# Transposed layouts from the host, tile order and buffers in a one-layer hybrid decoder kernel

## The chip, the cores and the metric

The kernel runs on 1 core of one Trainium2 chip. The metric is the device time of one execution in microseconds (us). A profiled execution gives the trace; its span runs from the first to the last instruction.

## The reference

One layer of a hybrid decoder trunk, for 1024 prompt tokens and 8 sample tokens with 4096 cached positions each; model width 1024, all in fp32.

```python
xn = rms_norm(x, norm1_g)
(aq, ak, av, az, ab, aa, bq, bk, bv, iq, ik, iw, ga, gb) = split(xn @ w_in)
# mixer A: causal conv of q, k, v (width 4), SiLU, chunked gated delta rule, gated norm -> oa
# mixer B: indexer scores, top 256 keys per query, softmax attention over them        -> ob
mix = sigmoid(ga) * (oa @ w_out_a) + sigmoid(gb) * (ob @ w_out_b)
h = x + mix @ w_o
hn = rms_norm(h, norm2_g)
y = h + square(relu(hn @ w_up)) @ w_down
```

It returns y, the new K/V and indexer rows, the recurrent state, and the last three rows ahead of the convolution (`conv_prompt`, `conv_sample`).

## The kernel before

Activations lie with channels on the 128 partitions and tokens along the free dimension, in three chunks of 384, 384 and 264 tokens (`CN`; tile t holds 128 tokens, t = 8 is the 8 samples, which stand at the end of chunk 2). Every fp32 operand is split into a high part in the fast fp32r format and a remainder (`split`), and each product is three matmuls. The kernel is written as chains (Python generators) that `Flow.run` interleaves; the planner of the tile framework (line 1867, it schedules with a simulated timeline) then sets the order on each engine. Nearly all loads and stores are issued by SyncE (SP), one queue in order. Since a wrapper issues every engine instruction, the profile gives them all line 83; they are told apart by tile name.

`mixers()` (line 400) comes first. `x_chain` (450) loads token tiles `xt` (two buffers) in the order samples, then 0 to 7; it squares them on ACT, takes the inverse root by Newton steps on VectorE (`rsqrt`, 177; 11 small operations with the mean), scales into a second tile `xs`, transposes (`ptx`, 8 per tile) and splits into `xn`. After the first tile it loads and splits the eight K/V weight blocks (`rawk`, `wk`). `kv_chain` (496) makes keys, values and indexer keys group by group, samples first, and then sets the event that lets the score work start. `dense_chain` runs the indexer queries (`iq_chain`, 938), the convolution part (`a_chain`, 570), queries, gates. `a_chain` transposes the convolution weights and the state on the chip (`ptc`, `pst`) and, at its end, the new convolution rows (`pcv`).

`rest()` (1602) comes second. `mix_a` (1543) projects mixer A's output and multiplies it with the gate, through DRAM (`gd`): for each of eight blocks and each chunk one load (1551), one product and one store (1553). `merge` (1566) follows for the chunks of `FIRST = [2, 0]`, beside the logits and values of the attention, and for `REST = [1]` after them: it loads the attention output (`load_b`, through DRAM), fetches x once more in token order as the residual, transposes it on TensorE (`ptx<-xt`, 8 per tile) and copies it by quarters into `hT` on VectorE and ACT (1572 to 1581); then come the products with `w_out_b` and `w_o`. While the attention runs, the products have one PSUM bank (`pd=1`, 1605). `norm_chain` and `mlp_chain` follow; after the last MLP block `out` (1788) transposes y back to token order (`pty`) and writes it.

Weight blocks come one after the other through `ahead` (1503) and `block` (205): 256 KB into a raw tile (two buffers of tag `raw`; from the MLP's stage on, every third block uses three buffers of tag `ld`, `cur["spare"]`), split by ACT and by VectorE or GpSimd in turn into one of five tiles.

Of the kernel before, what the change touches and what calls it, by code (L numbers as in the profile page):

```python
# [8 lines left out]
F32 = mybir.dt.float32  # L9
# [7 lines left out]
P = 128  # L17
D = 1024
# [12 lines left out]
FIRST, REST = [2, 0], [1]  # L31

# [93 lines left out]
def program(ctx, tc, I, O, dbg=None, upto=99):  # L126
# [78 lines left out]
    def block(src, name, lo="pool", spare=False):  # L205
# [4 lines left out]
        raw = w([P, 512], name + "r", tag="ld", bufs=3, pool=cur["L"]) if spare else \  # L210
# [10 lines left out]

    def cs(j):
        return slice(C0[j], C0[j] + CN[j])

    def dense(ws, xin, evac, chunks=range(3)):

        for j in chunks:
            p = pst("pdn", "pd")
# [117 lines left out]

    def q_rows(t, gt):
# [52 lines left out]
    def mixers():  # L400
# [49 lines left out]
        def x_chain():  # L450
# [9 lines left out]
            load(8)  # L460
            g1 = w([P, D], "g1")
            dma(g1, I["norm1_g"].to_broadcast([P, D]))
            load(0)
            wt["gt"] = gains(pools["A"])
            dma(gng, I["gdn_norm_g"].rearrange("a p -> p a"))
            wk = w([P, 2, KT, 336], "wk", F32R)
            for i, t in enumerate(order):
                n = NS if t == 8 else P
                x_ = xt[t]
                xs = w([P, D], "xs", bufs=2)  # L470
                ss = small([P, 1], "ss")
                S.activation(xs[:n], x_[:n], AF.Square, accum_out=ss[:n])
                V.tensor_scalar(ss[:n], ss[:n], 1.0 / D, EPS, op0=OP.mult, op1=OP.add)
                rs = small([P, 1], "rs")
                rsqrt(rs[:n], ss[:n])
                V.scalar_tensor_tensor(xs[:n], x_[:n], rs[:n], g1[:n], op0=OP.mult, op1=OP.mult)
                if i + 2 < 9:
                    load(order[i + 2])
                for j in range(2):
                    pt = pst("ptx", "px")  # L480
                    p3 = pt[:, :4 * n].rearrange("p (k n) -> p k n", k=4)
                    for k in range(4):
                        T.transpose(p3[:, k, :], xs[:n, (4 * j + k) * P:(4 * j + k + 1) * P], ident[:n, :n])
# [3 lines left out]
                if t == 8:  # L487
                    for k in range(KT):
                        raw = wts.tile([P, 512], F32, name="rawk", tag="raw", bufs=WB[1])
                        dma(raw[:, :336], I["w_kv"][:, k])  # L490
                        split(wk[:, 0, k], wk[:, 1, k], raw[:, :336], "act", "dve")
                    wt["kv"] = [wk[:, :, k] for k in range(KT)]
                    flow.set(ev_wkv)
# [76 lines left out]
        def a_chain():  # L570
            cur["p"] = pools["A"]
            cwr = w([48, P], "cwr", tag="j2", bufs=5, pool=C)
            dma(cwr, I["conv_w"][0].rearrange("j (t p) -> (j t) p", p=P))
            ptc = pst("ptc", "pt")
            T.transpose(ptc[:, :48], cwr, ident[:48, :48])
            cw = w([P, 4, 12], "cw")
            V.tensor_copy(cw, ptc[:, :48].rearrange("p (j t) -> p j t", j=4))
            stT = w([P, 12, 24], "stT")
            for g3 in range(3):
                scr = w([24, 512], "scr", tag="j2", bufs=5, pool=C)  # L580
                for j in range(3):
                    dma(scr[8 * j:8 * j + 8], I["state_conv"][0, :, j, g3 * 512:(g3 + 1) * 512])
                pt = pst("pst", "pt")
                for q in range(4):
                    T.transpose(pt[:, q * 24:(q + 1) * 24], scr[:, q * P:(q + 1) * P], ident[:24, :24])
                V.tensor_copy(stT[:, 4 * g3:4 * g3 + 4], pt[:, :96].rearrange("p (t x) -> p t x", t=4))
            dma(O["conv_sample"][0, :, 0:2, :], I["state_conv"][0, :, 1:3, :])
# [56 lines left out]
            for g3 in range(3):  # L644
                pcv = pst("pcv", "pt")
# [1233 lines left out]
```

## Time and profile before

| | us |
|---|---|
| median of 3 runs | 1876.12 |
| lowest, highest | 1874.29, 1876.82 |
| the profiled execution | 1872.74 |
| its span | 1870.9 |

The profile's page gives each engine's busy time, and the same in 40 slices of the span; stage tables, timelines and tile views are cut from the same trace. PE is TensorE's matmul, PEld its weight load, DVE VectorE, ACT ScalarE, POOL GpSimd, SP SyncE.

### The profile page before, as it was taken

What the parts mean: (1) busy time and instruction counts of PE and PEld (TensorE: products, weight loads), DVE (VectorE), ACT (ScalarE), POOL (GpSimd) and SP (SyncE); (2) the same over time, 40 slices, a digit from 0 to 9 for tenths busy, and PEclk for the clock granted to TensorE, in tenths of its full rate; (3) what the DMA queues carried; (4) which work ended last, traced back from release to release, by engine and by line L of the source; (5) the groups of instructions that cost most, each with busy time, mean ns of one, the idle gap of its engine ahead of it and who ended that gap; (6) DMA issues with size and microseconds to landing.
All of it is one profiled execution on the core that took longest, in us unless ns stands there. A gap on an engine that the chain in (4) does not pass through costs nothing.

```text
span 1870.9 us, 32909 instructions
## 1 busy us (share of the span) xinstructions
PE 1790.5 (96%) x11966; PEld 1715.5 (92%) x11966; DVE 1091.9 (58%) x2956; ACT 830.3 (44%) x1917; POOL 613.8 (33%) x765
## 2 busy tenths in 40 slices
PE   6999988899999999999899889999999999999998
PEld 4899978799898999989789889999999999999998
DVE  7868767998988896177778785323232323232323
ACT  4456684566687532256657544121313131313131
POOL 2434235613422362221443655121312131313130
PEclk9999999999999999999899999999999999999999
DMA  5325464225445444554654452111111111111112
GB/s 174 129 94 178 130 213 121 84 66 151 121 133 149 136 145 120 186 166 122 205 167 148 133 169 79 52 50 47 46 46 46 52 45 51 47 46 46 46 35 91
DMA packets 167764, 199.30 MB, mean 107 GB/s; under 512 B 29521, under 2 KB 112769, under 8 KB 167594
## 3 DMA queue, kind: packets, MB, share of 16 engines
q1 hardware_dynamic: 163314, 183.57, 32.4%
q0 software_dynamic: 4288, 13.64, 2.5%
q8 instruction: 94, 1.54, 0.3%
q14 instruction: 68, 0.56, 0.1%
HBM read 149.51 MB, written 47.73 MB: 105 GB/s over the span
## 4 chain that ended last, share of the span: by engine, by line
PE 45%; DMA 2%; DVE 2%; POOL 1%; issue 1%; ACT 0%; SPq 0%; ACTq 0%; POOLq 0%; DVEq 0%
PE pdn L83 42%; PE po L83 1%; PE ptp L83 1%; PE pat L83 1%; PE pty L83 0%; POOL wc L83 0%; DMA wc28r<-in_w_o 0%; DMA wc64r<-in_w_o 0%; DVE rs L83 0%; DVE wc L83 0%; DMA ld<-obd 0%; PE ptx L83 0%; DVE ga L83 0%; POOL ssq L83 0%; DMA wc58r<-in_w_b 0%
## 5 line engine op out<-in xcount | busy, mean ns | idle before, releaser
L83 PE MATMUL pdn<-u,wc 128*128 128x384 f32 (+1 forms) x2304 | 367.4, 320 | 0.0
L83 PEld LDWEIGHTS pdn<-u,wc 128*128 128x128 f32 x2304 | 362.8, 188 | 0.1
L83 PE MATMUL pdn<-hn,wc 128*128 128x384 f32 (+1 forms) x2304 | 362.1, 319 | 0.0
L83 PEld LDWEIGHTS pdn<-hn,wc 128*128 128x128 f32 x2304 | 360.5, 188 | 0.3
L83 DVE TENSOR_TENSOR hT<-hT,pdn 128x384 f32<-128x384 f32 (+1 forms) x216 | 110.5, 512 | 247.5 <-PE pdn L83 244.4
L83 PE MATMUL pdn<-xn,wu 128*128 128x384 f32 (+1 forms) x1440 | 250.8, 325 | 0.9 <-ACT z L83 0.9
L83 PEld LDWEIGHTS pdn<-xn,wu 128*128 128x128 f32 x1440 | 224.7, 189 | 9.1 <-issue 4.6
L83 DVE SCALAR_TENSOR_TENSOR r<-pdn,rs 128x384 f32<-128x384 f32 (+1 forms) x96 | 49.4, 515 | 273.6 <-PE pdn L83 273.5
L83 POOL TENSOR_TENSOR u<-r,u 128x384 fp32r<-128x384 f32 (+1 forms) x96 | 89.3, 931 | 274.1 <-ACT u L83 247.5
L83 PE MATMUL pa<-xn,wu 128*128 128x384 f32 (+1 forms) x864 | 160.2, 331 | 0.8 <-ACT a L83 0.8
L83 PEld LDWEIGHTS pa<-xn,wu 128*128 128x128 f32 x864 | 141.9, 195 | 3.2 <-ACT a L83 1.1
L83 ACT ACTIVATE r<-r 128x384 f32<-128x384 f32 (+1 forms) x96 | 47.1, 492 | 172.3 <-DVE r L83 171.6
L83 ACT ACTIVATE jka<-sc,nf 128x512 bf16<-128x512 f32 (+3 forms) x124 | 101.4, 822 | 27.0 <-DVE nf L83 21.5
L83 PE MATMUL pdn<-mix,wc 128*128 128x384 f32 (+1 forms) x576 | 100.6, 328 | 4.5 <-DVE wc L83 2.2
L83 PEld LDWEIGHTS pdn<-mix,wc 128*128 128x128 f32 x576 | 94.5, 194 | 7.8 <-ACT mix L83 2.6
L83 DVE SCALAR_TENSOR_TENSOR a<-u,cw,a 128x384 f32<-128x384 f32 (+1 forms) x108 | 76.0, 706 | 9.1 <-ACT a L83 8.1
L83 POOL TENSOR_TENSOR wu<-wu_4r,wu 128x512 fp32r<-128x512 f32 x32 | 42.2, 1318 | 92.6 <-ACT wu L83 77.7
L83 DVE TENSOR_SCALAR_CACHE_REDUCE jk<-sc,cf 128x768 bf16<-128x768 f32 (+1 forms) x62 | 66.1, 1072 | 1.8 <-ACT jka L83 1.7
L83 PE MATMUL pdn<-ob,wc 128*128 128x384 f32 (+1 forms) x288 | 54.7, 337 | 9.1 <-ACT ob L83 4.7
L83 PE MATMUL pqb<-wbq,xn 128*128 128x256 f32 (+1 forms) x432 | 59.1, 286 | 0.0
L83 ACT ACTIVATE lg<-lg,st 128x1024 f32<-128x1024 f32 (+7 forms) x64 | 49.3, 772 | 21.1 <-DVE st L83 19.7
L83 PEld LDWEIGHTS pdn<-ob,wc 128*128 128x128 f32 x288 | 46.9, 196 | 11.9 <-ACT ob L83 5.4
(905 smaller groups left out, 3284.0 us busy)
## 6 DMA issues: line engine op xcount, KB each, us to landing
wu_0r<-in_w_un SPq DMA_DIRECT2D x32, 256.0 KB
wu_4r<-in_w_un SPq DMA_DIRECT2D x32, 256.0 KB
gd<-g SPq DMA_DIRECT2D x32, 192.0 KB
ga<-gd SPq DMA_DIRECT2D x32, 192.0 KB
cqd<-a SPq DMA_DIRECT2D x24, 192.0 KB
xt<-in_x_prompt SPq DMA_DIRECT2D x8, 512.0 KB
obd<-rb SPq DMA_DIRECT2D x16, 256.0 KB
xt<-in_x_prompt SPq DMA_DIRECT2D x16, 256.0 KB
```

The source lines that it names most:

```text
L83: return f(*a, **k)
```

## The change

The host hands over x in transposed form too (`xT0` to `xT2`, one array for each chunk), and the convolution weights, the convolution state and the second norm's gain in the layout of the chip; it takes y and the new convolution rows transposed and turns them itself. In the kernel:

- Token tiles are normed in the order 0 to 7, then the samples; the K/V groups and the indexer queries have the samples last.
- `xt` has four buffers and is scaled in place; the gain is first scaled on GpSimd, and the Newton steps have two operations instead of three. The K/V weight blocks are loaded behind the first tile's scaling, into five buffers of another tag, with the remainder on GpSimd instead of VectorE.
- The residual is fetched straight into `hT`, two loads of four channel blocks for each chunk: for chunks 2 and 0 while `mix_a` runs (at m = 3 and m = 6), for chunk 1 in its merge at m = 4.
- In `rest()` every third weight block uses a third raw buffer (`raw2`), up to the MLP's stage.
- The last MLP block runs as the others do, and each block of y is written as soon as it has been added; `out` is gone.

```diff
+XO = (0, 1, 2, 3, 4, 5, 6, 7, 8)
+KVO = ([0, 1], [2, 3], [4, 5], [6, 7], [8])
+IQO = (2, 3, 4, 5, 6, 7, 8)
...
-        raw = w([P, 512], name + "r", tag="ld", bufs=3, pool=cur["L"]) if spare else \
+        raw = w([P, 512], name + "r", tag=spare[1], bufs=spare[2], pool=spare[0]) if spare else \
             wts.tile([P, 512], F32, name=name + "r", tag="raw", bufs=WB[1])
...
+    def residual(j, name):
+
+        hT[j] = w([P, 8, CN[j]], name, pool=cur["hp"])
+        for k in range(0, 8, 4):
+            dma(hT[j][:, k:k + 4], I[f"xT{j}"][:, k:k + 4])
...
-                xt[t] = w([P, D], "xt", bufs=2)
+                xt[t] = w([P, D], "xt", bufs=4)
...
-            load(8)
+            load(XO[0])
             g1 = w([P, D], "g1")
             dma(g1, I["norm1_g"].to_broadcast([P, D]))
-            load(0)
-            wt["gt"] = gains(pools["A"])
-            dma(gng, I["gdn_norm_g"].rearrange("a p -> p a"))
+            G.tensor_scalar(g1, g1, -1.0 / 8192, None, op0=OP.mult)
             wk = w([P, 2, KT, 336], "wk", F32R)
-            for i, t in enumerate(order):
+            for i, t in enumerate(XO):
                 n = NS if t == 8 else P
+                if i + 1 < 9:
+                    load(XO[i + 1])
                 x_ = xt[t]
-                xs = w([P, D], "xs", bufs=2)
-                ss = small([P, 1], "ss")
-                S.activation(xs[:n], x_[:n], AF.Square, accum_out=ss[:n])
+                sq = w([P, D], "sq", BF)
+                ss, z, u = (small([P, 1], x) for x in ("ss", "rs", "ru"))
+                S.activation(sq[:n], x_[:n], AF.Square, accum_out=ss[:n])
                 V.tensor_scalar(ss[:n], ss[:n], 1.0 / D, EPS, op0=OP.mult, op1=OP.add)
-                rs = small([P, 1], "rs")
-                rsqrt(rs[:n], ss[:n])
-                V.scalar_tensor_tensor(xs[:n], x_[:n], rs[:n], g1[:n], op0=OP.mult, op1=OP.mult)
-                if i + 2 < 9:
-                    load(order[i + 2])
+                V.tensor_scalar(z[:n].bitcast(I32), ss[:n].bitcast(I32), -0.5, 1597463007.0, op0=OP.mult, op1=OP.add)
+                for c in (3.0, 12.0, 768.0):
+                    V.scalar_tensor_tensor(u[:n], z[:n], ss[:n], z[:n], op0=OP.mult, op1=OP.mult)
+                    V.scalar_tensor_tensor(z[:n], u[:n], c, z[:n], op0=OP.subtract, op1=OP.mult)
+                V.scalar_tensor_tensor(x_[:n], x_[:n], z[:n], g1[:n], op0=OP.mult, op1=OP.mult)
+                if not i:
+                    for k in range(KT):
+                        raw = w([P, 512], "wkr", tag="j2", bufs=5, pool=C)[:, :336]
+                        dma(raw, I["w_kv"][:, k])
+                        split(wk[:, 0, k], wk[:, 1, k], raw, "act", "pool")
...
-                if t == 8:
-                    for k in range(KT):
-                        raw = wts.tile([P, 512], F32, name="rawk", tag="raw", bufs=WB[1])
-                        dma(raw[:, :336], I["w_kv"][:, k])
-                        split(wk[:, 0, k], wk[:, 1, k], raw[:, :336], "act", "dve")
...
-            for grp in ([8], [0, 1], [2, 3], [4, 5], [6, 7]):
+            for grp in KVO:
...
-            for g3 in range(3):
-                pcv = pst("pcv", "pt")
...
+            dma(O["conv_new"], ucol)
...
-                for t in [8] + list(range(2, 8)):
+                for t in IQO:
...
             held.append((m, blocks(1)))
+            if m in (3, 6):
+                residual(FIRST[m > 3], f"hT{FIRST[m > 3]}")
...
-            for t, c0, n in tokens(j):
-                for i in range(2):
-                    xt = w([P, 512], "xt", tag="ld", bufs=3, pool=cur["L"])
-                    dma(xt[:n], xrows((I["x_sample"], I["x_prompt"]), t)[:, 512 * i:512 * (i + 1)])
-                    pt = pst("ptx", "pt")
-                    for m in range(4):
-                        T.transpose(pt[:, m * P:m * P + n], xt[:n, m * P:(m + 1) * P], ident[:n, :n])
-                    for m in range(4):
-                        copy("act" if m % 2 else "dve", hT[j][:, 4 * i + m, c0:c0 + n], pt[:, m * P:m * P + n])
-                yield
+            yield
             for m in range(8):
                 ws = blocks(1)
+                if m == 4 and j in REST:
+                    residual(j, f"hT{j}")
...
+        cur["spare"], cur["hp"] = (M, "raw2", 1), M
...
-            cur["spare"] = True
+            cur["spare"], cur["hp"] = (st[5], "ld", 3), st[5]
...
-                for m in range(8 if g < 7 else 4):
-                    wd[m] = blocks(1)
-                    yield from down(m, chunks)
-            yield from out(chunks, 0)
-            for m in range(4, 8):
-                wd[m] = blocks(1)
-            for j in chunks:
-                for m in range(4, 8):
-                    yield from down(m, [j])
-                yield from out([j], 1)
...
+                for m in range(8):
                     def ev(j, c, p):
                         V.tensor_tensor(hT[j][:, m], hT[j][:, m], p, OP.add)
+                        if g == 7:
+                            dma(O["yT"][:, m, c], hT[j][:, m])
+                    yield from dense(blocks(1), lambda a, k, j: u[j][:, a, k], ev, chunks)
```

## Rows read from the trace of the kernel before

**Rows 1.** The page's head: the span, and each engine's busy time.
```profile
span 1870.9 us, 32909 instructions
PE 1790.5 (96%) x11966; PEld 1715.5 (92%) x11966; DVE 1091.9 (58%) x2956; ACT 830.3 (44%) x1917; POOL 613.8 (33%) x765
```
**Rows 2.** By stretch: length, engines' busy us (instructions), granted clock, DMA share, GB/s.
```profile
0.00:40.00 40.00, 21.50 (x128) 15.08 (x129) 29.05 (x105) 20.93 (x42) 9.49 (x31) 1.00 0.61 181
40.00:100.00 60.00, 56.42 (x427) 54.32 (x426) 48.87 (x167) 22.88 (x57) 23.50 (x29) 0.97 0.36 116
100.00:800.00 700.00, 670.51 (x4819) 629.85 (x4818) 543.61 (x1721) 410.01 (x1046) 270.64 (x414) 0.98 0.46 138
800.00:900.00 100.00, 92.21 (x573) 83.13 (x571) 78.09 (x204) 56.71 (x121) 21.85 (x30) 0.97 0.48 141
900.00:1110.00 210.00, 193.89 (x1209) 178.52 (x1209) 166.15 (x365) 128.83 (x299) 101.42 (x92) 0.97 0.55 166
1110.00:1835.00 725.00, 724.98 (x4604) 724.40 (x4603) 213.83 (x378) 186.26 (x345) 186.92 (x172) 1.00 0.16 49
1835.00:1871.00 36.00, 30.97 (x218) 30.22 (x216) 12.27 (x22) 4.69 (x9) 0.00 (x0) 0.98 0.31 118
```
**Rows 3.** The page's chain that ended last, shares of the span by engine.
```profile
PE 45%; DMA 2%; DVE 2%; POOL 1%; issue 1%; ACT 0%; SPq 0%; ACTq 0%; POOLq 0%; DVEq 0%
```
**Rows 4.** Timeline of the tail (start, us, engine); writes of y; stretch with pty alone.
```profile
1835.15 1.47 PE L83 MATMUL pty<-ident,hT 128*128 128x128 f32 x12
1864.69 0.55 DVE L83 TENSOR_TENSOR hT<-hT,pdn 128x384 f32<-128x384 f32 x1 [1.53 <-PE pdn L83]
1865.83 1.57 ACT L83 ACTIVATE yt<-pty 128x512 f32<-128x512 f32 x3 [5.29 <-PE pty L83]
...
L1796 SPq DMA_DIRECT2D out_y_prompt<-yt x16: 332/332/344, 1836.5 to 1867.4; - x16
...
1835.00:1871.00 36.00, 10.22 (x72) 8.27 (x72) 5.74 (x9) 4.69 (x9) 0.98 0.31 118
```
**Rows 5.** The merge: stretch with xt alone (PE, PEld, DVE, ACT); copies, ns min/median/max.
```profile
900.00:1110.00 210.00, 11.21 (x72) 8.51 (x72) 0.00 (x0) 0.00 (x0) 0.97 0.55 166
...
L83 DVE COPY hT<-ptx x36: 154/280/293, 903.4 to 1088.4; 128x128 f32<-128x128 f32 x32, 128x8 f32<-128x8 f32 x4
```
**Rows 6.** Convolution transposes by stretch: pcv (PE, PEld, ACT), then pst (PE, PEld, DVE).
```profile
360.00:390.00 30.00, 2.25 (x12) 1.29 (x12) 1.73 (x3) 0.94 0.33 97
...
0.00:100.00 100.00, 1.66 (x12) 1.32 (x12) 0.74 (x3) 0.98 0.46 142
```
**Rows 7.** Timeline of the head; then its small VectorE operations and K/V remainders by group.
```profile
2.69 1.05 ACT L83 ACTIVATE xs<-xt 8x1024 f32<-8x1024 f32 x1 [0.66 <-DMA xt<-in_x_sample]
6.65 1.06 ACT L83 ACTIVATE xs<-xt 128x1024 f32<-128x1024 f32 x1 [2.81 <-DMA xt<-in_x_prompt]
7.18 1.02 PE L83 MATMUL ptx<-ident,xs 8*128 8x8 f32 x8 [7.18 <-DVE xs L83]
11.76 1.53 DVE L83 SCALAR_TENSOR_TENSOR rs<-rs,rs 128x1 f32<-128x1 f32 x1
12.01 1.26 POOL L83 TENSOR_TENSOR wiq<-wiq_2r,wiq 128x512 fp32r<-128x512 f32 x1
15.29 1.97 PE L83 MATMUL ptx<-ident,xs 128*128 128x128 f32 x8 [0.57 <-DVE xs L83]
...
L83 DVE SCALAR_TENSOR_TENSOR rs<-rs,rs x33: 140/153/1535, 4.6 to 63.6; 128x1 f32<-128x1 f32 x24, 8x1 f32<-8x1 f32 x3, 8x2 f32<-8x2 f32 x3, 128x4 f32<-128x4 f32 x3
...
L83 DVE TENSOR_TENSOR wk<-rawk,wk 128x336 fp32r<-128x336 f32 x8 | 4.3, 539 | 1.3 <-ACT wk L83 1.3
```
**Rows 8.** By stretch, as rows 2: the strongest DMA load, and a stall of TensorE.
```profile
790.00:800.00 10.00, 6.85 (x40) 6.24 (x39) 6.00 (x9) 4.45 (x11) 7.05 (x10) 1.00 0.94 288
...
890.00:897.00 7.00, 2.18 (x10) 1.47 (x10) 3.06 (x11) 3.14 (x11) 2.21 (x3) 0.72 0.57 165
897.00:910.00 13.00, 10.99 (x58) 9.79 (x59) 7.14 (x21) 5.75 (x18) 6.39 (x8) 0.63 0.65 200
```

More of the change, by code (lines that the diff above doesn't have):

```diff
@@ L220, in unit, with dense @@
         return [x for k0 in range(0, src.shape[1], kt) for x in block(src[:, k0:k0 + kt], f"{name}_{k0}", lo)]
+    def residual(j, name):
+        hT[j] = w([P, 8, CN[j]], name, pool=cur["hp"])
+        for k in range(0, 8, 4):
+            dma(hT[j][:, k:k + 4], I[f"xT{j}"][:, k:k + 4])
     def cs(j):
         return slice(C0[j], C0[j] + CN[j])
-    def dense(ws, xin, evac, chunks=range(3)):
+    def dense(ws, xin, evac, chunks=range(3), tag="pd"):
         for j in chunks:
-            p = pst("pdn", "pd")
+            p = pst("pdn", tag)
             for k, wk in enumerate(ws):
@@ L345, in gains @@
         return gt
+    g2 = cst.tile([P, 8], F32, name="g2")
     def q_rows(t, gt):
@@ new lines, in x_chain @@
+                V.scalar_tensor_tensor(x_[:n], x_[:n], z[:n], g1[:n], op0=OP.mult, op1=OP.mult)
[4 more added lines that the diff above has]
+                        split(wk[:, 0, k], wk[:, 1, k], raw, "act", "pool")
+                    wt["kv"] = [wk[:, :, k] for k in range(KT)]
+                    flow.set(ev_wkv)
+                    wt["gt"] = gains(pools["A"])
+                    dma(g2, I["norm2_gT"])
+                    dma(gng, I["gdn_norm_g"].rearrange("a p -> p a"))
@@ L571, in a_chain @@
             cur["p"] = pools["A"]
[L572 to L575, printed above, removed]
             cw = w([P, 4, 12], "cw")
-            V.tensor_copy(cw, ptc[:, :48].rearrange("p (j t) -> p j t", j=4))
+            dma(cw, I["conv_wT"])
             stT = w([P, 12, 24], "stT")
-            for g3 in range(3):
[L580 to L587, printed above, removed]
+            dma(stT, I["stT"])
+            dma(O["conv_old"], I["state_conv"][0, :, 1:3, :])
             ucol = w([P, 12, NS + 3], "ucol")
@@ L643, in a_chain @@
                     flow.set(ev_k4 if i == 4 else ev_q4)
-            for g3 in range(3):
-                pcv = pst("pcv", "pt")
-                for q in range(4):
-                    T.transpose(pcv[:NS + 3, q * P:(q + 1) * P], ucol[:, 4 * g3 + q, :], ident)
-                cvo = w([NS + 3, 512], "cvo", tag="j2", bufs=5, pool=C)
-                copy("act", cvo, pcv[:NS + 3])
-                dma(O["conv_sample"][0, :, 2, g3 * 512:(g3 + 1) * 512], cvo[:NS])
-                dma(O["conv_prompt"][0, 0, :, g3 * 512:(g3 + 1) * 512], cvo[NS:])
+            dma(O["conv_new"], ucol)
             flow.set(ev_a)
@@ L1507, in ahead @@
             while todo and len(got) < depth[0]:
-                got.append(block(todo.pop(0), f"wc{i}", "pool" if i % 2 else "dve", cur["spare"] and i % 3 == 2))
+                got.append(block(todo.pop(0), f"wc{i}", "pool" if i % 2 else "dve", i % 3 == 2 and cur["spare"]))
                 i += 1
@@ L1848, in arrays_of @@
     a["qk_g"] = np.concatenate([gq, np.roll(gq, 32, 1), gk, np.roll(gk, 32, 1)], 1)
+    x = np.concatenate([np.asarray(inputs["x_prompt"])[0], np.asarray(inputs["x_sample"])[:, 0]])
+    for j, (c, n) in enumerate(zip(C0, CN)):
+        a[f"xT{j}"] = x[c:c + n].reshape(n, KT, P).transpose(2, 1, 0)
+    a["conv_wT"] = np.asarray(inputs["conv_w"])[0].reshape(4, 12, P).transpose(2, 0, 1)
+    a["stT"] = np.asarray(inputs["state_conv"])[0].reshape(NS, 3, 12, P).transpose(3, 2, 1, 0).reshape(P, 12, 24)
+    a["norm2_gT"] = np.asarray(inputs["norm2_g"])[0].reshape(8, P).T
     w = np.asarray(inputs["w_in"])[0]
@@ L1877 @@
     r = run_bass_kernel_spmd(nc, [arrays], core_ids=[0])
-    return tuple(r.results[0]["out_" + n] for n, _ in _OUTS)
+    return results_of(r.results[0])
```

45 lines of the change are left out of this document (12 added, 33 removed).

## The prediction

> **What bounds the kernel now.** I read the head of the page first, then a table by stage, then each stage with idle time or with work that the change touches. The head says that TensorE is busy 1790.5 of 1870.9 us [rows 1]. A busy share averages over stages, so I cut the span where the kernel changes its manner of work [rows 2]; subtracting TensorE's busy time from each stretch gives its idle time: 18.5 us in the first 40, 3.6 up to 100, 29.5 between 100 and 800, 7.8 between 800 and 900, 16.1 between 900 and 1110, none in the MLP (1110 to 1835), and 5.0 in the last 36. The chain that ended last is TensorE for most of its length, and where it is not it changes hands in short pieces between DMA, VectorE and GpSimd [rows 3]. So the kernel is TensorE's instruction stream with about 80 us of holes, half of them in places that the edits touch. Two kinds of saving are open: TensorE instructions that are removed where it is never idle (they count in full), and holes that are filled. VectorE is the second engine to watch: 166 of 210 us busy in the merge [rows 2].
>
> **The change part by part.**
>
> *The tail: y written channel by channel.* Before, 72 transposes bring y back to token order; from the first group at 1835.15 us they lie between the last matmuls [rows 4]. A matmul's price comes from the MLP, where TensorE has no hole: 724.98 us for 4604 of them, 0.1575 us each [rows 2]. The last stretch holds 4 blocks x 36 = 144 matmuls, 22.7 us. It has 30.97 us busy, so the transposes cost 8.3 us net (their own busy time, 10.22 us, overlaps the matmuls) [rows 2, 4]. The end changes too. Now the last addition into hT begins at 1864.69 us, 12 transposes follow, then three ACT copies of which the first begins at 1865.83, and the last write is issued at 1867.4; the span ends 3.5 us after that [rows 4]. After, the write follows the addition: 0.55 us of addition, and 3.5 us as the upper bound for issue and landing of a smaller write (192 instead of 256 KB). So the new end lies at 1835.15 + 22.7 + 0.55 + 3.5 = 1861.9, which is **9.0 us** earlier. Bounds: 8 if the 24 new writes of SP fall behind each other, 10.5 if the last write lands in about 2 us.
>
> *The merge: x fetched already transposed.* 72 transposes vanish from the merge. Their busy sum is 11.21 us [rows 5]; with the overlap that I found for the 72 equal ones of the tail the net price is 11.21 x 8.3/10.22 = 9.1 us. But TensorE is not the limit at every moment here, since 16.1 us are idle [rows 2]; I count **8 us**, with bounds 4 and 11.2. The 36 copies on VectorE (0.280 us, 10 us in all) vanish too [rows 5], and 36 on ACT. They stand in front of the weight splits and of the merge's products on in-order queues, and the third raw buffer lets one more weight block wait in SBUF. Of the 16.1 us of holes I give this **2 us** (bounds 0 and 5): most holes there wait for the attention output through DRAM, which is untouched.
>
> *The fetch itself.* hT of chunk 2 (264 tokens, 1.08 MB) and of chunk 0 (384, 1.57 MB) is now fetched in two steps each during the first half of the projection of A, and that of chunk 1 in its merge. The bytes are the same as before, the place is new: SP's queue also carries each step's load and store of the gate product, the raw weight blocks and the queries. 1.08 MB at the 288 GB/s that 790 to 800 us reached take 3.8 us, 1.57 MB take 5.5 [rows 8]. A load queued behind may be late by that much; TensorE has only one bank for this product in the stage (pd=1), so a late gate load stops the projection, while logits and values of other chains fill part of it. Nothing in the trace shows such a burst among the gate loads; bounds are 0 and the full 9.3 us, and I take **2 us lost**, near zero since 800 to 900 moves only 141 GB/s [rows 2].
>
> *The head.* Before, the 8 sample tokens go first, and the first prompt tile lands at 6.65 us but is transposed only at 15.29 [rows 7]. Unhindered, the chain from square to transposes takes 7.18 - 2.69 = 4.5 us, as the sample tile shows [rows 7]. After, tile 0 is first in SP's queue; with landing near 6 and this chain, it is transposed at about 10.5. The scaling of the gain row by GpSimd comes on top of nothing as long as it ends by then: a 128x512 operation there takes 1.26 us [rows 7], so about 2.5 for 1024, behind a load that is queued with tile 0. Then the stage is a matter of bytes: tiles 0 and 1, the gain and the eight K/V weight blocks are 2.9 MB, 16 us at the 181 GB/s of the first 40 [rows 2], so the first K/V product ends near 18 and TensorE still waits for tile 2 once. By estimate 10.5 idle us before the first transposes, 3 while the weights land and 2.5 before tile 2 make 16 in the first 40 instead of 18.5; with 2 us of removed convolution transposes (12 of them 1.66 us busy [rows 6]) that is **4 us**. With four tile buffers instead of two plus two, loads no longer wait for the normalisation; if that fills TensorE from 15 us on, it is 9 us, and if the bytes decide, 0. The samples aren't saved but moved to the end of each list; their K/V group now stands last before the score work may start, some microseconds of latency under dense work.
>
> [...] In the trace a 128x1 operation of VectorE with two SBUF inputs takes 1.53 us from 11.76, and ends at 13.29, when GpSimd's 128x512 subtraction of 12.01 + 1.26 ends; the median of its kind is 0.153 us [rows 7]. The change moves the eight K/V remainders, 8 x 0.54 us on VectorE, to GpSimd [rows 7]. At 336/512 of 1.26 us they take 0.83 each, 6.6 us in which the normalisation's small operations could be held, 2.3 us more than is taken off VectorE. The head's gain would be 1.7 instead of 4, inside my bounds. [...]
>
> *Convolution outputs.* The 12 transposes at 360 to 390 us (2.25 us busy [rows 6]) go, at the tail's net share **1.3 us** after rounding down; bounds 0 and 2.25.
>
> *Edits with one answer.* The convolution weights, state and second norm's gain are loaded ready-made: fewer small loads on SP and no operation of their own on any compute engine. Fewer Newton operations per tile (8 instead of 11 small VectorE operations, 0.15 us each) count within the head. The third raw buffer waits on a buffer, not on new work.
>
> **Sum.** 9.0 + 8 + 2 - 2 + 4 + 1.3 = 22.3 us, against the profiled execution's 1872.74 us (span 1870.9 and 1.8 around it): 1850.4, said as **1850**. The median of the three timed runs is 1876.12, 3.4 above the profiled one; I keep the profiled base, since the range is wider than that. A measurement of this kernel can tell about 0.2% (4 us) from no change.
>
> **The rivals.**
>
> *The merge stays VectorE's.* VectorE is 79% busy there [rows 2]. If what is removed from TensorE turns into waits for VectorE or for the attention output, the 8 + 2 us are lost: 1860. For it: the 16.1 us of holes. Against it: TensorE's own 193.9 us are still more than VectorE's, and VectorE loses 10 us itself.
>
> [...]
>
> *The whole order shifts.* The order on each engine is the planner's, so the 29.5 us of holes between 100 and 800 can grow or shrink without cause in one edit. I put it at 7 us either way around 1850.
>
> *The change doesn't do what it says in the head*: tiles come no sooner, because bytes bound it: 1854.
>
> [...]
>
> **How the numbers follow.** Forecast with shifts 0.64; merge stays VectorE's 0.11; more is won 0.13; head without gain 0.05; burst 0.07. The range takes in the bounds and reaches from "more is won" to just above "merge stays VectorE's" with an order shift of 7: 1836 to 1867. The first four cases are faster, less the tails of two of them: faster 0.88, same 0.06, slower 0.06.
>
> **What would show it.** Right: no transposes of x or y in the trace; from the start of the last four blocks to the end of the span 26.8 us instead of 35.8; the stretch of the merge loses 8 to 10 us; the first prompt transposes near 10.5 us; MLP unchanged at 725 us. Wrong: idle TensorE in the projection of A behind gate loads; the merge as long as before; or holes between 100 and 800 away from 29.5 by more than 10 us, which would make the total a matter of order and not of these terms.

## The result and the profile after

| | before | after |
|---|---|---|
| median, us | 1876.29 (4 runs, 1874.29 to 1876.82) | 1849.33 (4 runs, 1847.09 to 1853.85) |
| the profiled execution / its span | 1872.74 / 1870.9 | 1850.7 / 1848.6 |

The ratio is 0.9861, with a 95% interval of 0.9840 to 0.9882: faster by 1.4%. The forecast was 1850, and the two spans differ by 22.3 us, the sum of the prediction. That the sum came out is partly luck: two of its terms were right, and the errors of the others cancelled, as the sections below show.

The head of the page of after, answering [rows 1]:

```profile
span 1848.6 us, 32369 instructions
PE 1768.6 (96%) x11796; PEld 1699.7 (92%) x11796; DVE 1083.6 (59%) x2871; ACT 815.9 (44%) x1867; POOL 632.0 (34%) x774
```

TensorE is busy 21.9 us less (1790.5 to 1768.6), and its idle time is the same: 80.4 before, 80.0 after. Over the whole span, nothing was won by filling holes. They moved, as the stage table shows. It answers [rows 2]: stretch, its length, busy time and instructions of PE, PEld, DVE, ACT, POOL, granted clock, DMA share, GB/s.

```profile
0.00:40.00 40.00, 22.86 (x143) 21.67 (x144) 32.54 (x80) 23.72 (x48) 23.92 (x43) 1.00 0.69 218
40.00:100.00 60.00, 58.16 (x455) 55.57 (x454) 47.71 (x153) 23.59 (x59) 25.52 (x31) 1.00 0.38 120
100.00:800.00 700.00, 662.64 (x4731) 623.03 (x4730) 541.34 (x1716) 401.27 (x1030) 263.35 (x405) 0.98 0.45 133
800.00:900.00 100.00, 95.10 (x583) 85.24 (x581) 76.95 (x199) 56.17 (x119) 24.17 (x33) 0.98 0.53 168
900.00:1100.00 200.00, 184.92 (x1147) 170.47 (x1147) 168.70 (x341) 123.72 (x266) 105.84 (x93) 0.98 0.57 168
1100.00:1820.00 720.00, 719.71 (x4585) 718.79 (x4586) 209.12 (x373) 187.40 (x346) 189.15 (x173) 1.00 0.17 52
1820.00:1848.60 28.60, 25.20 (x160) 24.88 (x158) 7.26 (x14) 0.00 (x0) 0.00 (x0) 0.98 0.25 91
```

Fixed times mix stages once one kernel runs ahead of the other. So I cut both kernels at the same work: the first product of the projection of A (`pdn<-oa`), and the first product of the MLP (`pdn<-hn`). Ahead of the projection the cuts, 100 and 440 us, remain times. The columns are the same; first before, then after:

```profile
0.00:100.00 100.00, 77.92 (x553) 69.40 (x554) 77.91 (x270) 43.81 (x98) 32.98 (x60) 0.98 0.46 142
100.00:440.00 340.00, 318.16 (x2204) 302.07 (x2203) 270.35 (x731) 209.47 (x532) 132.91 (x241) 0.97 0.40 124
440.00:790.40 350.40, 345.90 (x2582) 321.94 (x2582) 267.26 (x982) 196.09 (x503) 130.68 (x164) 0.99 0.50 146
790.40:1134.30 343.90, 316.83 (x1952) 291.46 (x1951) 268.90 (x601) 202.05 (x455) 145.32 (x141) 0.97 0.53 159
1134.30:1870.90 736.60, 731.67 (x4683) 730.65 (x4681) 207.44 (x374) 178.90 (x331) 171.93 (x161) 1.00 0.16 50
```

```profile
0.00:100.00 100.00, 81.02 (x596) 77.24 (x597) 80.25 (x232) 47.32 (x107) 49.44 (x73) 1.00 0.50 159
100.00:440.00 340.00, 310.05 (x2098) 294.54 (x2097) 259.38 (x707) 197.99 (x511) 127.96 (x234) 0.95 0.39 118
440.00:794.60 354.60, 349.67 (x2620) 325.87 (x2620) 277.92 (x1003) 199.05 (x510) 131.55 (x166) 1.00 0.50 145
794.60:1124.10 329.50, 306.75 (x1878) 281.50 (x1877) 266.58 (x567) 198.76 (x422) 151.06 (x142) 0.98 0.55 167
1124.10:1848.60 724.50, 721.10 (x4612) 720.51 (x4610) 199.48 (x363) 172.75 (x318) 171.95 (x161) 1.00 0.17 51
```

Read the second number (the length) of the last two rows: the stage of the merge shrank by 14.4 us (343.9 to 329.5), the MLP with its end by 12.1 (736.6 to 724.5). Everything ahead of the projection of A became 4.2 us longer (790.4 to 794.6). It begins well, with 3.1 us less idle time by 100 us (22.1 to 19.0), and loses that between 100 and 440: 29.95 us idle instead of 21.84, at a mean granted clock of 0.95 instead of 0.97.

### The profile page after: what moved, and what is told of

Read it like the earlier page. It is cut to its first block, busy times and chain, and to the rows that moved or that the text cites. A ratio compares the mean times of both kernels' runs of the same rounds, so it can differ in the third digit from the quotient of the medians.

```text
span 1848.6 us, 32369 instructions
## 1 busy us (share of the span) xinstructions
PE 1768.6 (96%) x11796; PEld 1699.7 (92%) x11796; DVE 1083.6 (59%) x2871; ACT 815.9 (44%) x1867; POOL 632.0 (34%) x774
## 5 line engine op out<-in xcount | busy, mean ns | idle before, releaser
L86 PE MATMUL pdn<-u,wc 128*128 128x384 f32 (+1 forms) x2304 | 361.3, 318 | 0.0
L86 PE MATMUL pdn<-mix,wc 128*128 128x384 f32 (+1 forms) x576 | 95.2, 321 | 6.2 <-DVE hT L86 3.3
L86 PEld LDWEIGHTS pdn<-mix,wc 128*128 128x128 f32 x576 | 90.2, 188 | 9.7 <-DVE hT L86 3.7
L86 DVE SCALAR_TENSOR_TENSOR sc<-rl,wsg,sc 128x512 f32<-128x512 f32 (+1 forms) x70 | 52.5, 752 | 12.7 <-ACT rl L86 12.6
L86 PEld LDWEIGHTS pqb<-wbq,xn 128*128 128x128 f32 (+1 forms) x432 | 55.2, 182 | 3.4
```

The lines of the kernel that those rows point to most:

```text
L86: return f(*a, **k)
```

## The experiments

All kernels are the changed kernel with one edit (one has two). "A starts" is the time of the first `pdn<-oa`, "merge stage" runs from there to the first `pdn<-hn`, and "MLP" from there to the end of the span; these are from each kernel's profile. The ratio is to the kernel before, measured beside it: its medians there were 1874.45 us for e1 to e4, 1876.14 for e5 to e8 and 1875.07 for e9 to e12, so medians of different groups compare to about 2 us. A profile is one execution: that of e4 is the fastest of its five, 3.8 us under the median, and that of e12 is 3.0 above it.

| | median, us | ratio, 95% interval | A starts | merge stage | MLP |
|---|---|---|---|---|---|
| before | 1876.29 | 1 | 790.4 | 343.9 | 736.6 |
| after | 1849.33 | 0.9861 [0.9840, 0.9882] | 794.6 | 329.5 | 724.5 |
| e1 old tail | 1858.53 | 0.9911 [0.9891, 0.9931] | 791.6 | 329.6 | 734.0 |
| e2 old residual | 1864.90 | 0.9940 [0.9924, 0.9956] | 792.6 | 346.5 | 724.7 |
| e3 two raw buffers | 1852.67 | 0.9878 [0.9860, 0.9896] | 791.4 | 334.4 | 724.5 |
| e4 samples first | 1840.15 | 0.9816 [0.9800, 0.9833] | 780.8 | 329.3 | 724.5 |
| e5 samples second | 1855.80 | 0.9896 [0.9878, 0.9913] | 801.2 | 327.8 | 724.5 |
| e6 queries last | 1849.39 | 0.9860 [0.9841, 0.9879] | 791.4 | 330.0 | 724.5 |
| e7 other order | 1849.64 | 0.9855 [0.9838, 0.9871] | 795.0 | 330.4 | 724.4 |
| e8 K/V on VectorE | 1847.17 | 0.9844 [0.9830, 0.9859] | 790.5 | 330.7 | 724.4 |
| e9 only transposes | 1855.62 | 0.9897 [0.9875, 0.9918] | 789.5 | 338.3 | 724.5 |
| e10 only copies | 1850.53 | 0.9866 [0.9845, 0.9887] | 792.1 | 332.3 | 724.5 |
| e11 fetch in merge | 1846.05 | 0.9850 [0.9827, 0.9873] | 793.5 | 325.4 | 724.4 |
| e12 e4 and e8 | 1837.01 | 0.9799 [0.9780, 0.9818] | 782.4 | 331.4 | 724.5 |

Two columns carry the argument. The MLP is 724.4 to 724.7 us in every kernel that has the new end, so it can be compared to a few tenths of a us from one profile each. The merge stage is coarser. In after, e1, e4, e5, e6, e7, e8 and e12 TensorE issues the same instructions in the same order from the projection of A to the MLP, and takes 327.8 to 331.4 us, mean 329.8: one profile tells little of a difference under 3 us. "A starts" is coarser still: after, e1, e2, e3, e9, e10 and e11 issue the same TensorE instructions in the same order up to there, and reach it at 789.5 to 794.6, mean 792.2.

One rival stays untested in the merge. With each of e2, e3, e9, e10 and e11 the planner also changes TensorE's order there, and no run changes that order alone. By the medians only e2 among these five is clear of after; the intervals of the other four overlap its own.

### The end of the kernel

e1 puts back the two halves of the last MLP block and the transposes of y:

```diff
-                        if g == 7:
-                            dma(O["yT"][:, m, c], hT[j][:, m])
-                    yield from dense(blocks(1), lambda a, k, j: u[j][:, a, k], ev, chunks)
+            yield from out(chunks, 0)
...
+            for j in chunks:
+                for m in range(4, 8):
+                    yield from down(m, [j])
+                yield from out([j], 1)
```

> The changed kernel with only the old end: the last MLP block in two halves and y turned to token order by 72 transposes on TensorE. Theory (a TensorE instruction that is removed where TensorE is never idle counts in full): the stretch from the start of the last four blocks to the end of the span grows by 9 to 12 us, so 1858 to 1861 against 1849.3 of the changed kernel; everything ahead of the last MLP block stays as it is. Rival (the transposes ran under the last matmuls and their weight splits, and the gain of the change is elsewhere): under 3 us, 1849 to 1852.

Measured: 1858.53, and the MLP row of its stage table is

```profile
1121.20:1855.20 734.00, 728.95 (x4684) 727.93 (x4682) 205.06 (x372) 177.43 (x327) 171.87 (x161) 1.00 0.16 50
```

The old end costs 9.5 us (734.0 against 724.5), 7.85 of it busy time of TensorE. The theory holds, and the rival is out. The last instructions of after show the rest (timeline: start, duration, engine, operation):

```profile
1842.76 2.44 PE L86 MATMUL pdn<-u,wc 128*128 128x384 f32 x13
1845.24 0.56 DVE L86 TENSOR_TENSOR hT<-hT,pdn 128x384 f32<-128x384 f32 x1 [1.55 <-PE pdn L86]
```

The span ends 2.8 us after this addition (1845.80 to 1848.6), where the prediction allowed 3.5, and in its upper bound about 2 for the landing, which no run shows. From the start of the last 144 matmuls, at 1822.5, to the end of the span are 26.1 us; the prediction had named 26.8 as its sign of being right, against 35.8 before.

### The merge, in four pieces

e2 brings the old residual back, with the third raw buffer kept. e9 and e10 take it apart: the transposes alone, and the copies alone. e3 removes the third raw buffer, e11 moves the fetch.

```diff
 e2: the 72 transposes and 72 copies of before, residual() not called
 e9:
+                    pt = pst("ptx", "pt")
+                    for m in range(4):
+                        T.transpose(pt[:, m * P:m * P + n], ident[:n], ident[:n, :n])
 e10:
+                    T.matmul(pt[:, :2], ident, ones[:, :2], start=True, stop=True)
+                    for m in range(4):
+                        e = "act" if m % 2 else "dve"
+                        copy(e, w([P, P], "d" + e)[:, :n], pt[:, :1].to_broadcast([P, n]))
 e3:
-        cur["spare"], cur["hp"] = (M, "raw2", 1), M
+        cur["spare"], cur["hp"] = False, M
 e11:
-            if m in (3, 6):
-                residual(FIRST[m > 3], f"hT{FIRST[m > 3]}")
...
-                if m == 4 and j in REST:
+                if m == 4:
```

> The changed kernel with the residual fetched in token order in the merge again, 72 transposes on TensorE and 72 copies on VectorE and ACT; the third raw buffer stays. Theory (removed TensorE work is what the merge gained): 8 to 9 us slower, 1857 to 1858, and TensorE's idle time between 790 us and the MLP about as in the changed kernel. Rival 1 (VectorE bounds the merge, so its 10 us of copies come on top): 14 us or more, 1863 or above. Rival 2 (the transposes sit in holes and the third raw buffer made the gain): under 3 us, at most 1852.

> The changed kernel without the third raw buffer up to the MLP's stage (two raw buffers as before the change). Theory: the buffer is worth 0 to 5 us, 2 by my estimate, 1849 to 1854, since the holes of this stretch wait for the attention output. Rival 2 (the third buffer made the merge's gain, which was 14 us against the 8 forecast): 6 to 10 us slower, 1855 to 1859, with TensorE waiting for weight blocks between 900 and 1120 us.

> The changed kernel with 72 transposes of the identity added in the merge, where the residual's stood, and their results not read; the residual comes as in the changed kernel. The stage from the projection of A to the MLP took 329.6 us in the changed kernel and 346.7 with the old residual. Theory (the residual cost TensorE's own time, and waiting for its copies and loads on top): 4 to 6 us here, half of that or more of it in TensorE's work, idle time and clock as in the changed kernel, so 1853 to 1856. Rival (TensorE's work is all): 8 to 9 us or more, 1857 or above.

> The changed kernel with the residual's 72 copies added in the merge (36 on VectorE and 36 on ACT, 128x128 from a PSUM bank into scratch tiles that nobody reads; each four fed by a product of two columns), without the 72 transposes and without the old loads. Theory (the removed copies on the in-order queues made the 4 us of idle time and the 5 us of clock loss): the stage grows by 6 to 10 us, nearly all of it idle time and clock loss, so 1855 to 1860. Rival (VectorE and ACT have room for them, and the loads of x in the merge made it): under 3 us, at most 1852.

> The changed kernel with the residual of chunks 2 and 0 fetched in their merges (at m = 4, as that of chunk 1) and not during the projection of A. If the fetch delays gate loads there (my 2 us lost, bounds 0 and 9.3): the projection of A gets up to 2 us shorter, 1847 to 1849. If it delays nothing: within 1 us of 1849.3, or slower by up to 4 us when the additions into hT then wait for the fetch in the merge.

The row of the merge stage in the stage tables of e2, e9, e10, e3 and e11, to be read against 329.50 and 306.75 of after:

```profile
792.60:1139.10 346.50, 320.03 (x1950) 294.34 (x1950) 271.85 (x603) 204.65 (x458) 148.39 (x142) 0.96 0.52 159
```
```profile
789.50:1127.80 338.30, 315.97 (x1951) 288.75 (x1950) 268.50 (x567) 197.61 (x422) 149.47 (x142) 0.98 0.53 163
```
```profile
792.10:1124.40 332.30, 310.48 (x1914) 284.29 (x1913) 274.46 (x601) 203.54 (x455) 148.09 (x141) 0.98 0.54 165
```
```profile
791.40:1125.80 334.40, 309.05 (x1877) 283.00 (x1877) 269.56 (x566) 197.40 (x421) 148.54 (x142) 0.98 0.54 164
```
```profile
793.50:1118.90 325.40, 306.98 (x1879) 284.19 (x1878) 267.05 (x567) 197.14 (x422) 147.03 (x142) 0.97 0.55 169
```

*Transposes.* Alone they cost 8.8 us of stage (0.12 us each; 8.5 against the mean of the eight), 9.2 of busy time, and no idle time. My expectation for e9 (4 to 6) was too low and its rival's 8 to 9 right; so was the prediction's 8 with the net price of 9.1.

*Copies.* Alone they cost 2.8 us, 0.9 more than the longest of the eight, with 3.7 us more busy time, which includes the 18 small products that feed them. They run at the length they had in [rows 5] (groups by form, busy us and mean ns of one behind the bar):

```profile
L86 DVE COPY ddve<-ptx 128x128 f32<-128x128 f32 x32 | 9.1, 286 | 1.5 <-ACT dact L86 0.9
```

9 us of VectorE's time, in a stage where it is busy 81%, cost about 2.8: the theory of e10 (6 to 10) is wrong, and its rival (under 3) holds. VectorE's work as a whole does not bound the merge. Single results of it are nevertheless what TensorE waits for: of the waits listed for this stage 19.6 of 21.8 us end on VectorE in after, 12.3 of 26.5 in before.

*The old residual as a whole* costs 17.0 us (346.5), 5.4 more than transposes and copies by themselves. As e2 also takes the new fetch out of the projection of A, and fetching later wins 4.1 in e11 below, the old residual itself may cost up to 9.5 more than the two. What remains is the token-order loads, the chain from load over transpose to copy, and the other order. A part shows in the waits of TensorE in that stage of e2 (waiting tile, releaser: us in total, times, longest):

```profile
PE ptx L86 <- DMA xt<-in_x_prompt: 2.8, 3, 1.3
```

The other 2.6 to 6.7 us I can't assign. The theory of e2 (8 to 9) is too small; the size is that of its rival 1, but e10 takes away the cause that rival 1 gave.

*The third raw buffer* is worth 4.9 us of stage (334.4, which is 3.0 more than the longest of the eight); the medians differ by 3.3, with intervals that overlap. It is more than my 2, within the theory's 5 and below the rival's 6 to 10. That it works by having the next weight block ready is not shown: TensorE's waits for split weights (tile `wc`) are 2.4 us in after and 2.0 in e3. Nor is it shown to depend on the new residual: e2 has the buffer and the old residual, before has neither, and e2's stage is the longer by 2.6 us (346.5 against 343.9), which one profile each can't tell.

*The fetch.* With the call in the merges, the stage is 4.1 us shorter (325.4, which is 2.4 less than the shortest of the eight). The medians agree (3.3 us), though their intervals overlap. This is twice my 2 and inside its bounds, but that the fetch delays the projection is not shown. The first product of the merge (`pdn<-mix`) comes 142.7 us after the projection's start in e11, and 142.5 to 145.9 in the eight kernels: up to there e11 is within their spread, and what it wins beyond them it wins later, where TensorE's order differs too. The code's place (m = 3 and 6) does not tell when the fetch is issued. The operations on tile hT, after first, then e11 (first and last start in us):

```profile
L229 SPq DMA_DIRECT2D hT<-in_xT x4: 327/422/465, 800.7 to 807.9; - x4
```
```profile
L229 SPq DMA_DIRECT2D hT<-in_xT x4: 423/450/753, 811.3 to 815.1; - x4
```

The planner issues all four loads 6 to 13 us after the projection began, among the first gate and weight loads; that it does so as soon as their buffers exist is my reading. Moving the call into the merge put them only 7 to 11 us later, still well inside the projection, whose last product starts at 896.4 in e11; so e11 does not test the projection without the fetch, as its expectation meant to. In the 20 us from 795, after moves 319 GB/s and e11 252, yet TensorE is idle for 4.5 and 4.3 us there.

### The order of tiles and samples

```diff
 e4: XO = (8, 0, 1, ..., 7);  KVO = ([8], [0, 1], ...);           IQO = (8, 2, ..., 7)
 e5: XO = (0, 1, 8, 2, ...);  KVO = ([0, 1], [8], [2, 3], ...);   IQO = (8, 2, ..., 7)
 e6: XO and KVO as e4;                                            IQO = (2, ..., 7, 8)
 e7: order as after;  in Flow.Eng:  c = 0.065  ->  c = 0.075
```

> The changed kernel with the samples first again in the three lists (tiles, K/V groups, indexer queries); the four tile buffers, the scaling in place and the order of loads stay. Theory (samples last make the sample chain, the score chain and the gate chains begin together at 140 us, which costs about 10 us between 100 and 440): that stretch loses 6 to 10 us of idle time and clock loss, and the first prompt transposes come 2 to 4 us later, so 1842 to 1847. Rival (the 10 us there are only another order of the planner without a cause in the samples): the idle time between 100 and 440 stays near 26 us, or moves without pattern, and the time is 1849 to 1854.

> The changed kernel with the samples early but not first: tiles 0, 1, samples, 2 to 7; K/V groups [0, 1], samples, then the others; indexer queries with the samples first. Theory (samples that end last make several chains start together at 140 us): the stretch from 100 to 440 us is as in the kernel with the samples first (idle about 21 us instead of 26, clock loss about 9 instead of 15), and the first prompt transposes stay near 13.4 us, so 1836 to 1842. Rival (the gain of the samples-first kernel was a lucky order): idle and clock loss of that stretch as in the changed kernel, 1847 to 1853.

> The changed kernel with the samples first in the tiles and in the K/V groups, but last in the indexer queries as the change has it. If the K/V group of the samples as the last one is the cause (the score work's start waits for it): as the samples-first kernel, 1838 to 1843. If the indexer queries of the samples are the cause (their sample scores wait for them): as the changed kernel, 1847 to 1852.

> A control: the changed kernel with one constant of the order's cost table (0.065 for a transpose) set to 0.075; the same instructions, interleaved a little differently. If orders shift without a cause in the samples: the stretch from 100 to 440 us differs from the changed kernel's 26 us idle and 15 us clock loss by 5 us or more, and the time is up to 7 us off 1849, either way. If the stretch is set by what is last in the lists: within 3 us of 1849.

e4 came out on the theory's side and faster than it said (1842 to 1847): 1840.15, below the changed kernel with intervals that don't overlap. Its idle time from 100 to 440 us is 20.77 us against 29.95 in after (by the stage table; the 26 in the expectations is not what it shows), and its first prompt transposes come at 18.11 us instead of 13.44. e5 then broke the theory: its samples are early too, and it is slower than e4 by 15.7 us and slower than its rival said. The two rows from 100 us to the projection of A, e4 first, then e5:

```profile
100.00:440.00 340.00, 319.23 (x2196) 304.40 (x2195) 279.80 (x730) 206.30 (x529) 137.69 (x243) 0.97 0.40 127
440.00:780.80 340.80, 337.05 (x2550) 313.82 (x2549) 266.39 (x977) 193.42 (x499) 125.33 (x159) 1.00 0.49 147
```
```profile
100.00:440.00 340.00, 316.17 (x2170) 301.74 (x2169) 269.87 (x723) 208.94 (x539) 136.35 (x240) 0.96 0.41 125
440.00:801.20 361.20, 350.90 (x2572) 327.37 (x2571) 268.50 (x981) 192.28 (x490) 126.45 (x163) 0.97 0.48 140
```

The counts in these rows differ by what has been postponed; up to the projection all the changed kernels issue the same 5310 TensorE instructions. From 100 to 440 us e5 is idle for 23.83 us, nearer to e4 than to after, so its loss lies behind. Between 440 us and the projection, e4 is idle 3.8 us at a clock of 1.00, e5 10.3 us at 0.97; by my estimate the lower clock costs e5 another 11 us (0.03 x 361.2). TensorE's waits there name single late operations in e5, which e4 has not:

```profile
PE pkS L86 <- DVE St L86: 4.2, 1, 4.2
PE pks L86 <- DMA Ss<-in_state_ssm: 2.7, 1, 2.7
```

Thus the order of three short lists moved the start of the projection between 780.8 and 801.2 us with the same instructions; the seven profiles of one order differ by 5.1. e6, with the indexer queries of the samples last, loses e4's gain, so that list matters in this order; e7, the control, is the changed kernel's time again, with 3.8 us less idle time from 100 to 440 and 3.7 more behind. Samples first was fast in both kernels that have it in all three lists (e4, e12: 780.8, 782.4), samples last was slow in after, e7 and e8 (790.5 to 795.0). But before has the samples first in all three too, and starts the projection at 790.4, with other instructions ahead of it. Whether the samples themselves do it, or these orders happen to collide less, is open: e5 speaks against a rule.

### The head

```diff
 e8:
-                        split(wk[:, 0, k], wk[:, 1, k], raw, "act", "pool")
+                        split(wk[:, 0, k], wk[:, 1, k], raw, "act", "dve")
 e12: e8 with the lists of e4
```

> The changed kernel with the remainders of the eight K/V weight blocks on VectorE again instead of GpSimd. Theory (VectorE's small operations with two SBUF inputs are held while GpSimd works): the small operations behind the gain's scaling take 0.15 us again, the first prompt transposes come at 10.5 to 12 us instead of 13.44 (the gain's scaling on GpSimd stays), TensorE's idle time in the first 40 us falls by 1 to 2 us, and the time is 1846 to 1849. Rival (the eight operations of 0.5 us on VectorE now stand ahead of the normalisation of tiles 1 and 2 instead): first 40 us as long or longer, 1849 to 1851.

> The changed kernel with the samples first again and the K/V remainders on VectorE, the two edits that were faster than it alone (1840.15 and 1847.17). If the gains add: 1838. If the gain of the samples-first order is only that order's own luck: any other order gives its own idle time and clock loss between 100 and 800 us, so 1838 to 1850, and TensorE's work without idle time and clock loss stays at 1742 to 1746 us as in all kernels with these instructions.

The timeline of the head of after, answering [rows 7] (start, duration, engine, operation, and in brackets the idle time before and who ended it):

```profile
4.50 1.06 ACT L86 ACTIVATE sq<-xt 128x1024 bf16<-128x1024 f32 x1 [2.46 <-DMA xt<-in_x_prompt]
6.25 2.80 POOL L86 TENSOR_SCALAR g<-g 128x1024 f32<-128x1024 f32 x1 [2.95 <-DMA g<-in_norm_g]
6.31 1.00 DVE L86 SCALAR_TENSOR_TENSOR rs<-ru,rs 128x1 f32<-128x1 f32 x1
8.04 0.16 DVE L86 SCALAR_TENSOR_TENSOR rs<-ru,rs 128x1 f32<-128x1 f32 x1
9.19 0.15 DVE L86 TENSOR_SCALAR ss<-ss 128x1 f32<-128x1 f32 x1 [0.98 <-ACT sq L86]
9.70 5.30 POOL L86 TENSOR_TENSOR wk<-wkr,wk 128x336 fp32r<-128x336 f32 x5 [0.66 <-ACT wk L86]
9.81 0.80 DVE L86 SCALAR_TENSOR_TENSOR rs<-ru,rs 128x1 f32<-128x1 f32 x1
10.65 0.82 DVE L86 SCALAR_TENSOR_TENSOR ru<-rs,ss 128x1 f32<-128x1 f32 x1
11.39 1.99 DVE L86 SCALAR_TENSOR_TENSOR xt<-xt,rs,g 128x1024 f32<-128x1024 f32 x1
13.44 1.97 PE L86 MATMUL ptx<-ident,xt 128*128 128x128 f32 x8 [13.44 <-DVE xt L86]
```

Tile 0's root is ready at 8.2 and the gain at 9.05, so its scaling could end by 10.4: the prediction's 10.5. It starts at 11.39, since the planner queued the mean and root of tile 1 (from 9.19) ahead of it on VectorE, and two of those small operations take 0.80 and 0.82 us while GpSimd computes K/V remainders. It then lasts 1.99 us, again beside GpSimd. Tile 0 itself had landed by 4.50, sooner than the prediction's 6; from its square to the transposes are 8.9 us instead of 4.5. e8 takes the remainders off GpSimd (same view):

```profile
10.46 0.50 DVE L86 TENSOR_TENSOR wk<-wkr,wk 128x336 fp32r<-128x336 f32 x1
10.88 0.15 DVE L86 SCALAR_TENSOR_TENSOR rs<-ru,rs 128x1 f32<-128x1 f32 x1
11.36 1.28 DVE L86 SCALAR_TENSOR_TENSOR xt<-xt,rs,g 128x1024 f32<-128x1024 f32 x1
12.70 1.97 PE L86 MATMUL ptx<-ident,xt 128*128 128x128 f32 x8 [12.70 <-DVE xt L86]
```

With GpSimd idle (in e8 from 9.13 to 13.48 us) the same scaling takes 1.28 us and the small operation that took 0.80 takes 0.15, but the transposes come at 12.70, not at 10.5 to 12, since tile 1's operations are still ahead. In after the scaling starts 2.3 us later than the gain allows and lasts 0.7 longer than in e8, so the queue's order was the greater part. The 0.74 us between the two kernels is not the whole effect of GpSimd: in e8 tile 1 landed later, and its mean starts at 9.95 us instead of 9.19. Counted from that mean, the transposes come after 4.25 us in after and 2.75 in e8. TensorE's idle time in the first 40 us fell by 1.3 (17.14 to 15.85), as expected; the median's 2.2 us less lie within the intervals. e12 was the fastest kernel of this study, 1837.01, 12 us below the changed kernel with intervals that don't overlap; the gains of e4 and e8 would have added to 1838. But its interval overlaps e4's, so that the gains add is not shown.

## Why the prediction was right, and where it was not

| term | forecast, us | measured | from |
|---|---|---|---|
| tail | 9.0 (8 to 10.5) | 12.1; alone 9.5 | stage tables; e1 |
| transposes of the merge | 8 (4 to 11.2) | 8.8 | e9 |
| copies and third raw buffer | 2 (0 to 5) | 2.8 + 4.9 | e10, e3 |
| fetch in the projection of A | -2 (0 to -9.3) | -4.1 against a later fetch | e11 |
| merge stage in all | 8 | 14.4 | stage tables |
| head and convolution outputs | 5.3 | -4.2 | A starts at 794.6 |
| sum | 22.3 | 22.3 | spans |

*Tail: right.* The term, put back alone, is 9.5 us. Before and after differ by 2.6 more in the MLP, since before's MLP is slower than e1's (736.6 against 734.0) with the same products. TensorE's order there is the same too. Matched one by one, the starts of the matmuls in the two traces drift apart only in the second products of the MLP (`pdn<-u`, 2.7 us over 2304 of them) and by 0.1 us in the first (`pdn<-hn`); the cause is open. But for this the MLP did not change, as said.

*Merge: the transposes right, the rest mis-sized.* The transposes' price, taken from the tail's overlap, was right to 0.8 us. Mis-sized was "copies and third raw buffer": e10 and e3 give 7.7 where I gave 2 with an upper bound of 5. The reading behind it was wrong: I had said that most of the 16.1 us of holes wait for the attention output (tile `ob`). TensorE's waits between 900 and 1110 show 1.7 us on it, and 5.4 on split weights (`wc`). Three lines of the waits in the whole merge stage of before, then three of after (waiting tile, releaser: us in total, times, longest):

```profile
PE pdn L83 <- ACT ob L83: 4.7, 2, 3.1
PE pdn L83 <- ACT wc L83: 2.9, 2, 1.8
PE pdn L83 <- DVE wc L83: 2.5, 2, 2.2
```
```profile
PE pat L86 <- DVE qS L86: 4.5, 3, 2.9
PE pdn L86 <- DVE wc L86: 2.4, 2, 2.2
PE pdn L86 <- ACT ob L86: 0.4, 1, 0.4
```

The waits for weights did fall, but neither e3 (2.0) nor e10 (2.5) brings them back. Only the old residual as a whole (e2, 4.6) lies beyond the 2.2 to 3.7 of the eight kernels with one order, so what filled these holes stays open. The pieces sum to 12.4 of the 14.4 us; the difference is within the spread of the stage. The rival "the merge stays VectorE's" is out: the stage lost 14.4 us, and e10 shows that VectorE's copies are not its price, though more of the waits that are left end on VectorE than before. The rival that more is won (0.13) counted on the stall from 890 to 910 us in [rows 8]. It came true in part there, but the stall also moved. These are the same two stretches in after:

```profile
890.00:897.00 7.00, 7.00 (x52) 6.68 (x51) 6.27 (x21) 3.81 (x12) 1.82 (x3) 1.00 0.69 204
897.00:910.00 13.00, 9.44 (x63) 8.85 (x61) 9.39 (x24) 7.93 (x22) 6.73 (x7) 0.87 0.69 203
```

Over the 20 us TensorE is idle for 3.6 us instead of 6.8, at a granted clock that fell less, to 0.87 where it was 0.63; as the projection starts 4.2 us later in after, the two windows do not hold quite the same work. The range's lower end, 1836, takes 9 us for this place, about half of it for the lower clock; that half was my estimate and no run shows it. What the runs show is 3.2 us less idle time there, and the whole stage 14.4 us shorter. Two thirds of the 14.4 us are busy time (316.83 to 306.75), a third is idle time (27.1 to 22.75).

*Fetch: the price stays open.* I gave 2, and a fetch 7 to 11 us later makes the stage 4.1 us shorter; but no run does without the fetch and keeps the rest, and that it delays gate loads, as I had argued, is not shown. I also took the code's place for the queue's. The chance of 0.07 for a burst that makes the kernel slower counted on losses through the clock as well; they were my estimate, and no run shows them. The stage became 14.4 us shorter, at a granted clock of 0.98 instead of 0.97.

*Head: the step that failed* is the unhindered chain of 4.5 us from square to transposes. The planner put the next tile's small operations ahead, and the tile's scaling, ready at 9.05, waited behind them; the chain took 8.9 us. The idle time of the first 40 us, forecast at 16, was 17.1, partly by luck: the tile landed 1.5 us sooner than I had assumed. By 100 us after has 3.1 us less idle time than before, so the loss of 4.2 in the table is made behind that point. That a VectorE operation can take longer beside GpSimd, as one does in [rows 7], after and e8 show again: 0.80 us beside GpSimd and 0.15 without it, 1.99 and 1.28. Not every such operation does: of the small ones during the gain's scaling in after (6.25 to 9.05) only the one at 6.31 took 1.00, and the last, at 8.04, took 0.16. On the first transposes e8 shows the effect as 0.74 us (13.44 to 12.70), and as 1.5 counted from tile 1's mean; I had worked out 2.3.

*Order between 100 and 800: the term I had no price for.* The rival "the whole order shifts" had 7 us either way. From 785.1, which the forecast's 5.3 us give for the start of the projection, after is 9.5 away and the seven executions of its order 7.1 on the mean. Its idle time from 100 to 800 is 37.4 instead of 29.5, within the 10 us that I set. So errors cancelled: 9.5 lost ahead of the projection, 3.1 and 6.4 gained in the tail and the merge beyond the forecast.

## What to carry to other kernels

Where TensorE has few holes, price a removed instruction by the net of a stretch (length, not its own busy time): that gave 9 and 8 us to within one. Where an automatic planner orders the work, cut both traces at the same work, not at the same time, and try a few orders of any short list before drawing a conclusion: here an order was worth more (up to 16 us) than most edits. Before reading a difference of 3 us from one profile each, look how far profiles of the same order differ in that stage. Look up on the queue, not in the code, when a prefetch is issued.

## What the runs showed of the hardware

- In the MLP, where TensorE is idle for 3.4 of 724.5 us in after, its time repeats to 0.1 us from kernel to kernel: 724.4 or 724.5 us in 11 of the 12 kernels with the new end, 724.7 in e2. But before and e1, whose TensorE order is the same there too, differ by 2.6 us (736.6 and 734.0). One TensorE order spreads over 789.5 to 794.6 us at the projection of A, and over 327.8 to 331.4 us in the merge stage; these stages have holes (53.9 us idle ahead of the projection and 22.75 in the merge stage of after, by the stage table).
- TensorE's idle time and a lower granted clock come together in some stretches and not in others. In e5 10.3 us of idle time between 440 and 801 us come with a granted clock of 0.97, which by the estimate above costs about as much again; in e4 3.8 us come with 1.00, and in the first 100 us of after 19.0 us come with 1.00.
- In the head of after, up to 16 us, a VectorE operation on 128 single numbers with two input tiles takes 0.15 to 0.22 us, and 0.80 to 1.20 in six cases, all beside a GpSimd operation; scaling a 128x1024 tile takes 1.99 beside GpSimd there and 1.28 in e8 with GpSimd idle. Not every such operation beside a GpSimd operation takes longer: the one at 8.04 us in after takes 0.16.
